# A diffusion-transformer trunk in float32: the last layer's second MLP product by Strassen's scheme of seven half products, with the residual transposed early and three of the products kept in PSUM

## The chip, the cores and the metric

The kernel runs on one core of a Trainium2 chip. A core has five engines with instruction streams of their own: PE (TensorE, the matrix unit), DVE (VectorE), ACT (ScalarE), POOL (GpSimd) and SP (SyncE, which here issues the DMAs). Tiles live in SBUF (128 partitions) and matmul results in PSUM. The metric is the device time of one execution in microseconds. The profile is that of one execution; its times are microseconds from its first instruction.

## The reference, cut to what matters

```python
def sqrelu_mlp(h, w1, w2):
    return jnp.square(jax.nn.relu(h @ w1)) @ w2
...
    for i in range(DEPTH):
        ...
        x = x + gx1 * y_x
        ...
        x = x + gx2 * sqrelu_mlp(modulate(rmsnorm(x, norm2_g[i]), sx2, ax2), w_mlp1[i], w_mlp2[i])
    return x
```

There are two layers, 512 latent tokens and a width of 1024; the MLP's hidden width is 4096. In the last layer only the latent tokens go through the MLP, and its result is the output (512 x 1024, token by row). The change lies in that last layer: in the product of the squared activations (512 x 4096) with `w_mlp2` (4096 x 1024), the gate `gx2` and the residual sum.

## The kernel before

Each product is taken in float32 accuracy from three matmuls. An operand is split into a high part, rounded to the matrix unit's format (`split`: ACT copies it, line 76), and a low part, the rest (DVE or POOL subtracts, line 77). Then high x high, high x low and low x high are added in PSUM (`mm3`, lines 109 to 111; `fm_block` runs it over the depth). A weight slab is a 1 MB DMA on SP into a raw tile (`r_w`, `load_slab`, line 90), then two ACT copies of 128x1024 into `h_w` and two subtractions of 128x1024 into `l_w`. The pool of these high and low parts has two buffers each.

The activations `X` are kept feature by partition, token by column. The last layer's MLP goes over the hidden width in four chunks of 1024. For each chunk:

- `hidden`, the first product (tiles `f`): four slabs of 256 hidden features, each two blocks of 24 matmuls with 512 tokens as columns. ACT takes relu (L1250), the square as high part `fh` (L1251) and the square (L1252), DVE the low part `fl` (L1253).
- `out_slabs`, the second product (tiles `r`): four slabs of 256 output features, each two blocks of 24 matmuls; the weights are the stationary operand. DVE adds gate x result to `X` (L1171).

So a chunk is 192 matmuls of `f` and 192 of `r`, and PE goes from one to the other without a pause. In the last layer the low parts of these weights are taken by DVE; POOL is not used in this MLP once the second norm is done. In the last chunk each `r` slab is followed by `after`: eight transposes to token by row (tiles `oT`, L1306), copies by DVE and ACT, and four DMAs to the output (L1313).

The first chunk begins while the second norm (`norm_mod`) is still at work on the second half of the tokens: ones-matmul `nc_n` (L331) sums the squares over partitions, DVE and POOL make the factor (`ms_n`, `dg_n`), the matmul `nb_n` (L320) spreads it, and from this DVE, ACT and POOL make the normed half (`nu_n`, `h2h`, `h2l`). Slabs 0 and 1 of the first chunk are therefore computed in halves of 256 tokens, the first halves of both slabs first:

```python
for s0 in ((0, 2), (2, 3), (3, 4)) if cch == 0 else ((n, n + 1) for n in range(4)):
    ...
    for g in halves if cch == 0 and s0[0] == 0 else groups:
```

The program is written as straight code; a scheduler places each instruction in its engine's stream, and an engine works its stream in order.

## Time and profile before

| | |
|---|---|
| three runs of the kernel before | 2336.35, 2337.66 and 2341.13 us, median 2337.66 |
| span of the profiled execution | 2337.3 us |
| granted clock of PE in it | 0.994 |
| last layer's MLP, first `f` matmul to the span's end | 1973.13 to 2337.3 us |
| last `r` phase, first matmul to the span's end | 2284.85 to 2337.3 us |

In a row of the timeline the columns are the start, the length, the engine, the line, the operation, and output <- inputs by the program's names; "xN" joins N like rows, whose length is then that from the first one's start to the last one's end. In brackets stands the time that the engine was idle before it, and what ended that. In a grouped row the columns behind the bar are busy us and mean ns of one, then the idle time ahead of the group. A matmul's length is that of its whole way through the array: the next one starts before it ends, so the distance from start to start is what one costs. In the table of windows each engine has its busy time with the number of its instructions in brackets, and behind them stand PE's granted clock, DMA's busy share and GB/s.

### The profile page before, as it was taken

The numbers are of one execution on the slowest core, as the hardware profiler recorded it, in microseconds if no ns is written. First come the engines' busy times: TensorE is split into PE (matmuls) and PEld (weight loads), VectorE is DVE, ScalarE is ACT, GpSimd is POOL, SyncE is SP. The second block draws the span as 40 slices with busy tenths as digits, with TensorE's granted clock in tenths as the row PEclk, the third lists the DMA queues.
The fourth block names the chain that finished last, engine by engine and source line by source line (L and its number), as shares of the span: only waits on it lengthen the run. The fifth ranks groups of instructions, "written<-read, shape, count | busy, mean of one in ns | idle before, by whom it ended". The sixth has DMA issues, their size and how long they took to land.

```text
span 2337.3 us, 36377 instructions
## 1 busy us (share of the span) xinstructions
PE 2272.6 (97%) x14626; PEld 2036.2 (87%) x14626; DVE 1488.6 (64%) x2586; ACT 996.0 (43%) x1967; POOL 681.8 (29%) x789
## 2 busy tenths in 40 slices
PE   8999999999999999999999999999999999999999
PEld 6999998888888998888888998999877779888887
DVE  6777776599657445555656567867759965433333
ACT  5555655522333362332415255655543334432432
POOL 1866764110000143232323266757510000000000
PEclk9999999999999999999999999999999999999999
DMA  9211111134544223333334311111114324223222
GB/s 305 61 36 45 46 46 45 46 129 142 175 139 165 65 82 120 124 109 126 122 113 128 108 46 57 44 44 44 62 41 160 115 88 127 90 91 106 92 91 72
DMA packets 222570, 224.76 MB, mean 96 GB/s; under 512 B 6256, under 2 KB 212544, under 8 KB 222272
## 3 DMA queue, kind: packets, MB, share of 16 engines
q1 hardware_dynamic: 222400, 222.43, 29.5%
q8 instruction: 115, 1.88, 0.3%
q14 instruction: 55, 0.45, 0.1%
HBM read 208.73 MB, written 13.67 MB: 95 GB/s over the span
## 4 chain that ended last, share of the span: by engine, by line
PE 78%; DVE 11%; POOL 4%; ACT 3%; DMA 2%; issue 2%; SPq 0%; POOLq 0%; DVEq 0%; ACTq 0%
PE r L109 6%; PE r L111 6%; PE r L110 6%; PE f L109 6%; PE f L110 6%; PE f L111 6%; DVE cacc L974 3%; PE qk L109 2%; PE qk L110 2%; PE qk L111 2%; PE gt L109 2%; PE gt L110 2%; PE gt L111 2%; PE o L109 2%; PE o L110 2%
## 5 line engine op out<-in xcount | busy, mean ns | idle before, releaser
L110 PE MATMUL f<-h2l,h_w 128*128 128x512 f32 (+1 forms) x832 | 282.7, 341 | 1.3 <-POOL h2l L77 1.3
L109 PE MATMUL f<-h2h,h_w 128*128 128x512 f32 (+1 forms) x832 | 281.7, 342 | 2.2 <-ACT h2h L76 1.7
L109 PE MATMUL r<-fh,h_w 128*128 128x512 f32 (+1 forms) x832 | 283.2, 341 | 0.1
L110 PE MATMUL r<-fl,h_w 128*128 128x512 f32 (+1 forms) x832 | 283.0, 340 | 0.0
L111 PE MATMUL r<-fh,l_w 128*128 128x512 f32 (+1 forms) x832 | 282.9, 340 | 0.0
L111 PE MATMUL f<-h2h,l_w 128*128 128x512 f32 (+1 forms) x832 | 281.3, 340 | 0.0
L77 POOL TENSOR_TENSOR l_w<-r_w,h_w 128x1024 fp32r<-128x1024 f32 x64 | 157.1, 2476 | 336.8 <-ACT h_w L76 336.8
L76 ACT ACTIVATE h_w<-r_w 128x1024 fp32r<-128x1024 f32 x128 | 128.6, 1052 | 225.4 <-PE r L110 117.2
L974 DVE SCALAR_TENSOR_TENSOR cacc<-z,cols,cacc 128x783 f32<-128x783 f32 (+1 forms) x240 | 207.8, 917 | 0.3
L1171 DVE SCALAR_TENSOR_TENSOR X<-r,ad,X 128x512 f32<-128x512 f32 (+1 forms) x104 | 65.1, 626 | 190.3 <-PE r L111 190.0
L109 PE MATMUL qk<-h_wqk,h1h 128*128 128x256 f32 x640 | 183.3, 289 | 2.1 <-ACT rw L566 1.3
L110 PE MATMUL qk<-l_wqk,h1h 128*128 128x256 f32 x640 | 180.7, 285 | 0.0
L111 PE MATMUL qk<-h_wqk,h1l 128*128 128x256 f32 x640 | 176.9, 285 | 0.3 <-POOL h1l L77 0.3
L1253 DVE TENSOR_TENSOR fl<-fr,fh 128x512 fp32r<-128x512 f32 (+1 forms) x104 | 77.3, 746 | 155.7 <-ACT fr L1252 155.5
L110 PEld LDWEIGHTS f<-h2l,h_w 128*128 128x128 f32 x832 | 157.5, 189 | 20.1 <-POOL h2l L77 2.4
L109 PEld LDWEIGHTS f<-h2h,h_w 128*128 128x128 f32 x832 | 156.6, 189 | 21.1 <-ACT h2h L76 2.3
L109 PEld LDWEIGHTS r<-fh,h_w 128*128 128x128 f32 x832 | 157.7, 190 | 17.7 <-DVE X L1171 0.3
L111 PEld LDWEIGHTS r<-fh,l_w 128*128 128x128 f32 x832 | 157.7, 190 | 17.7
L110 PEld LDWEIGHTS r<-fl,h_w 128*128 128x128 f32 x832 | 157.8, 190 | 17.4
L111 PEld LDWEIGHTS f<-h2h,l_w 128*128 128x128 f32 x832 | 157.2, 189 | 17.6
L738 DVE TENSOR_REDUCE st<-S 128x1 f32<-128x768 f32 (+1 forms) x160 | 134.4, 845 | 57.9 <-PE S L736 56.7
L279 DVE SCALAR_TENSOR_TENSOR adaac<-ar,cvec,adaac 128x256 f32<-128x256 f32 x336 | 156.5, 529 | 20.4 <-ACT adaac L276 15.5
(256 smaller groups left out, 6281.8 us busy)
## 6 DMA issues: line engine op xcount, KB each, us to landing
r_w<-in_w_mlp_dram SPq DMA_DIRECT2D x64, 1024.0 KB, 5.3
ada<-in_w_ada_dram SPq DMA_DIRECT2D x24, 1024.0 KB, 5.6
ar<-in_w_ada_dram SPq DMA_DIRECT2D x48, 512.0 KB, 3.6
r_wqk<-in_w_in_dram SPq DMA_DIRECT2D x32, 512.0 KB, 5.1
r_wg<-in_w_in_dram SPq DMA_DIRECT2D x16, 1024.0 KB, 5.4
r_wv<-in_w_in_dram SPq DMA_DIRECT2D x8, 1024.0 KB, 5.2
r_wao<-in_w_attn_out_dram SPq DMA_DIRECT2D x8, 1024.0 KB, 4.8
r_wo<-in_w_out_dram SPq DMA_DIRECT2D x8, 1024.0 KB, 8.8
```

The source lines that it names most:

```text
L76: nc.scalar.activation(out=hi, in_=src, func=AF.Copy)
L77: return (lo_eng or nc.vector).tensor_tensor(out=lo, in0=src, in1=f32(hi), op=ALU.subtract)
L109: nc.tensor.matmul(ps, sh, mh, start=first, stop=False)
L110: nc.tensor.matmul(ps, sh, ml, start=False, stop=False)
L111: nc.tensor.matmul(ps, sl, mh, start=False, stop=last)
L279: nc.vector.scalar_tensor_tensor(out=a[:, q], in0=r[:, j], scalar=cvec[:, k, q : q + 1], in1=a[:, q], op0=ALU.mult, op1=ALU.add)
L738: nc.vector.tensor_reduce(out=st[:, m : m + 1], in_=S[:, :nkey], axis=AX.X, op=ALU.max, negate=True)
L974: nc.vector.scalar_tensor_tensor(out=ca[cc][:, :CV], in0=zt[cc][:, t : t + CV], scalar=wcol, in1=ca[cc][:, :CV], op0=ALU.mult, op1=ALU.add)
L1171: state["done"] = nc.vector.scalar_tensor_tensor(out=X[:, mb, g], in0=ps[:, :W], scalar=gate[:, s, mb : mb + 1], in1=X[:, mb, g], op0=ALU. ...
L1253: state["done"] = nc.vector.tensor_tensor(out=fl[mb][:, g], in0=r[:, :W], in1=f32(fh[mb][:, g]), op=ALU.subtract).ins
```

## The change

For the last layer a new function `last_mixing` takes the place of the loop over chunks. A chunk's second product is A (512 tokens x 1024 hidden) times B (1024 hidden x 1024 outputs). Both are cut in two by two: A11, A12, A21, A22 are halves by tokens and by hidden features (each slab's first block of 128 goes to the first half, its second to the second), and B's quarters `b11`, `b12`, `b21`, `b22` are loaded by one 1 MB DMA each (rows of 512 columns, four raw buffers). Instead of eight half products there are seven, in the Winograd form: with S1 = A21 + A22, S2 = S1 - A11, S3 = A11 - A21, S4 = A12 - S2 and T1 = b12 - b11, T2 = b22 - T1, T3 = b22 - b12, T4 = b21 - T2 they are product 1 = A11 b11, 2 = A12 b21, 3 = S4 b22, 4 = A22 T4, 5 = S1 T1, 6 = S2 T2 and 7 = S3 T3. Their order is 1, 5, 6, 3, 7, 2, 4. Each is two blocks (128 tokens each) of 24 matmuls of 512 columns, so a chunk has 168 matmuls in place of 192. The activations are now the stationary operand, and the result comes out token by row.

- DVE makes the four sums of activations for each slab (`sm`, 128x256 each, L500 to L503) and the low parts of A11 (`aol`) and of the second block (in `h2hl`, unused columns of the old `h2l` tile); ACT copies the high parts, and POOL subtracts the low parts of the four sums (128x1024).
- DVE makes T1 (L559), T2 (L561), T3 (L562) and T4 (L564) in the raw tiles, 128x2048 each.
- `halves_of` splits each of the seven right operands: ACT copies two halves of 128x1024, DVE subtracts the first half and POOL the second.
- Products 1, 5, 6 and 7 are added over the chunks into quarters of `X` (L533, after the first chunk with one operand in PSUM); 3, 2 and 4 stay in PSUM over the four chunks.
- The residual `X` is transposed in the first chunk (`turn_x`, 32 transposes at L476, copies at L480 and L482, eight DMAs of 256 KB to `xt_d`) and read back at the end; the gate comes as a row for all partitions (`grow`) through DRAM.
- At the end DVE joins the products (L590 to L608), applies the gate (L586) and adds the residual (L587), POOL does the latter two for one quarter, and the last quarter is done in `u` tiles (L616, L617; three buffers) of 256 columns. The outputs go out by ten DMAs (L546, L618).
- In the first chunk only slab 0 is computed in halves of 256 tokens, and block by block instead of half by half.

What the function replaces in the chunk loop (`after` with its transposes and `out_slabs` for the last layer) is left out of the diff:

```diff
+    def last_mixing(fp, mi_, mc, X, h2, h2hl, L, w1):
...
+        def turn_x(n):
+            t, h = n // 2, n % 2
+            ps = mi_.tile([P, 512], F32, tag="mi", name=f"xT{n}")
+            for k in range(4):
+                nc.tensor.transpose(ps[:, k * P : k * P + P],
+                                    X[:, 4 * h + k, t * P : t * P + P], ident)
+            o = state["xp"].tile([P, 512], F32, tag="u", bufs=3, name=f"xt{n}")
...
+            nc.sync.dma_start(xt_d[t, h], o)
+
+        def hidden(c, s):
...
+            for m in range(2):
+                for g in (LAT,) if c or s else (slice(0, 256), slice(256, 512)):
...
+                    nc.scalar.activation(out=fr[:, m, g], in_=ps[:, :W], func=AF.Relu)
+                    nc.scalar.activation(out=fr[:, m, g], in_=fr[:, m, g], func=AF.Square)
+            sm = fp.tile([P, 4, HP], F32, tag="sm", name=f"sm{c}_{s}")
+            a11, a21, a12, a22 = fr[:, 0, :HP], fr[:, 0, HP:], fr[:, 1, :HP], fr[:, 1, HP:]
+            tt = nc.vector.tensor_tensor
+            split(AB[0][:, 0, s], AB[1][:, 0, s], a11)
+            tt(out=sm[:, 0], in0=a21, in1=a22, op=ALU.add)
+            tt(out=sm[:, 2], in0=a11, in1=a21, op=ALU.subtract)
+            tt(out=sm[:, 1], in0=sm[:, 0], in1=a11, op=ALU.subtract)
+            tt(out=sm[:, 3], in0=a12, in1=sm[:, 1], op=ALU.subtract)
+            split(AT[0][:, :, s], AT[1][:, :, s], fr[:, 1].rearrange("p (o n) -> p o n", o=2))
+            split(AB[0][:, 1:, s], AB[1][:, 1:, s], sm, nc.gpsimd)
+
+        def quarter(c, kh, nh):
+            r = fp.tile([P, HK, HN], F32, tag="raw", bufs=4, name=f"r_w2_{c}_{kh}{nh}")
...
+        def halves_of(r, name):
+            hi = wpool.tile([P, HK, HN], F32R, tag="whi", name=f"h_{name}")
+            lo = wpool.tile([P, HK, HN], F32R, tag="wlo", name=f"l_{name}")
+            for k, eng in ((slice(0, 2), nc.vector), (slice(2, 4), nc.gpsimd)):
+                split(hi[:, k], lo[:, k], r[:, k], eng)
+            return hi, lo
+
...
+        tt = nc.vector.tensor_tensor
+        kept = {}
+
+        def summed(n, c, a, w):
+            for t in range(2):
+                ps = mm_tile(f"r{c}_{n}_{t}")
+                product(ps, a, w, t, True, True)
+                if c:
+                    tt(out=M[n][:, t], in0=M[n][:, t], in1=ps, op=ALU.add)
+                else:
+                    nc.vector.tensor_copy(M[n][:, t], ps)
+
+        def held(n, c, a, w, t):
+            if c == 0:
+                pool, tg = (mc, "mc") if n == 2 else (mi_, "mi")
+                kept[n, t] = pool.tile([P, 512], F32, tag=tg, name=f"r_{n}_{t}")
+            product(kept[n, t], a, w, t, c == 0, c == 3)
+            return kept[n, t]
+
...
+        quarters = Y.rearrange("p t (h n) -> p h t n", h=2)
+        M = {n: quarters[:, q // 2, 2 * (q % 2) : 2 * (q % 2) + 2]
+             for q, n in enumerate((1, 5, 6, 7))}
+        for c in range(4):
+            for s in range(4):
+                hidden(c, s)
+                if c == 0:
+                    turn_x(2 * s)
+                    turn_x(2 * s + 1)
+            b22, b12, b21, b11 = (quarter(c, *q) for q in ((1, 1), (0, 1), (1, 0), (0, 0)))
+            summed(1, c, A11, halves_of(b11, f"b11_{c}"))
+            tt(out=b11, in0=b12, in1=b11, op=ALU.subtract)
+            summed(5, c, S1, halves_of(b11, f"t1_{c}"))
+            tt(out=b11, in0=b22, in1=b11, op=ALU.subtract)
+            tt(out=b12, in0=b22, in1=b12, op=ALU.subtract)
+            summed(6, c, S2, halves_of(b11, f"t2_{c}"))
+            tt(out=b11, in0=b21, in1=b11, op=ALU.subtract)
+            w22 = halves_of(b22, f"b22_{c}")
+            if c < 3:
+                for t in range(2):
+                    held(3, c, S4, w22, t)
+                summed(7, c, S3, halves_of(b12, f"t3_{c}"))
+                w21 = halves_of(b21, f"b21_{c}")
+                for t in range(2):
+                    held(2, c, A12, w21, t)
+                wt4 = halves_of(b11, f"t4_{c}")
+                for t in range(2):
+                    held(4, c, A22, wt4, t)
+                continue
+
+            gn = [grow[:, :HN], grow[:, HN:]]
+            xt = []
+            for q in range(2):
+                r = fp.tile([P, 2, 2, 512], F32, tag="raw", bufs=4, name=f"xr{q}")
+                nc.sync.dma_start(r, xt_d[2 * q : 2 * q + 2].rearrange("t h p n -> p t h n"))
+                xt.append(r)
+
+            def gated(tq, nq, t, v, eng=nc.vector):
+                eng.tensor_tensor(out=v, in0=v, in1=gn[nq], op=ALU.mult)
+                eng.tensor_tensor(out=v, in0=v, in1=xt[tq][:, t, nq], op=ALU.add)
+
+            for t in range(2):
+                tt(out=M[6][:, t], in0=M[1][:, t], in1=M[6][:, t], op=ALU.add)
+            for t in range(2):
+                ps = held(3, c, S4, w22, t)
+                v = state["xp"].tile([P, 512], F32, tag="u", bufs=3, name=f"c12_{t}")
+                tt(out=v, in0=M[5][:, t], in1=ps, op=ALU.add)
+                tt(out=v, in0=M[6][:, t], in1=v, op=ALU.add)
+                gated(0, 1, t, v)
+                put(0, 1, t, v)
+            summed(7, c, S3, halves_of(b12, f"t3_{c}"))
+            for t in range(2):
+                tt(out=M[7][:, t], in0=M[6][:, t], in1=M[7][:, t], op=ALU.add)
+                tt(out=M[5][:, t], in0=M[7][:, t], in1=M[5][:, t], op=ALU.add)
+                gated(1, 1, t, M[5][:, t], nc.gpsimd)
+                put(1, 1, t, M[5][:, t])
+                gated(1, 0, t, M[7][:, t])
+            w21 = halves_of(b21, f"b21_{c}")
+            for t in range(2):
+                ps = held(2, c, A12, w21, t)
+                tt(out=M[1][:, t], in0=M[1][:, t], in1=ps, op=ALU.add)
+                gated(0, 0, t, M[1][:, t])
+                put(0, 0, t, M[1][:, t])
+            wt4 = halves_of(b11, f"t4_{c}")
+            for t in range(2):
+                ps = held(4, c, A22, wt4, t)
+                for j, o in enumerate((slice(0, 256), slice(256, 512))):
+                    u = state["xp"].tile([P, 512], F32, tag="u", bufs=3, name=f"u{t}_{j}")[:, :256]
+                    tt(out=u, in0=ps[:, o], in1=gn[0][:, o], op=ALU.mult)
+                    tt(out=u, in0=u, in1=M[7][:, t, o], op=ALU.add)
+                    nc.sync.dma_start(out[0, (2 + t) * P : (3 + t) * P, o], u)
...
```

Where the change moves instructions, three places show it. First, the product phase of the second chunk. On DVE, before, in the phase of the third chunk (names: `l_w2` low parts of the weights, `fl` low parts of the activations, `r` the second product's blocks):

```order
L77 TENSOR_TENSOR l_w2_1_2_0_22193<-r_w2_1_2_0_22190,h_w2_1_2_0_22192 128x1024 x2
L1253 TENSOR_TENSOR fl1_2_5_21913<-fr1_2_5_0_22117,fh1_2_5_21912 128x512
L1253 TENSOR_TENSOR fl1_2_6_21915<-fr1_2_6_0_22155,fh1_2_6_21914 128x512
L77 TENSOR_TENSOR l_w2_1_2_1_22253<-r_w2_1_2_1_22250,h_w2_1_2_1_22252 128x1024 x2
L1253 TENSOR_TENSOR fl1_2_7_21917<-fr1_2_7_0_22185,fh1_2_7_21916 128x512
L1171 SCALAR_TENSOR_TENSOR X2_20128<-r1_2_0_0_22198,ad1_9372,X2_20128 128x512
L1171 SCALAR_TENSOR_TENSOR X2_20128<-r1_2_1_0_22224,ad1_9372,X2_20128 128x512
L77 TENSOR_TENSOR l_w2_1_2_2_22313<-r_w2_1_2_2_22310,h_w2_1_2_2_22312 128x1024 x2
L1171 SCALAR_TENSOR_TENSOR X2_20128<-r1_2_2_0_22258,ad1_9372,X2_20128 128x512
```

and after, in the phase of the second chunk (`r_w2_1_00`, `01`, `10`, `11` are the raw quarters b11, b12, b21, b22, overwritten by T1, T2, T4 in the first and T3 in the second; `fr1_3` are slab 3's activations, `r1_n_t` a block of product n):

```order
L503 TENSOR_TENSOR sm1_2_21606<-fr1_2_21551,sm1_2_21606 128x256
L559 TENSOR_TENSOR r_w2_1_00_21697<-r_w2_1_01_21693,r_w2_1_00_21697 128x2048
L562 TENSOR_TENSOR r_w2_1_01_21693<-r_w2_1_11_21691,r_w2_1_01_21693 128x2048
L77 TENSOR_TENSOR aol_20749<-fr1_3_21625,aoh_20748 128x256
L501 TENSOR_TENSOR sm1_3_21680<-fr1_3_21625 128x256
L77 TENSOR_TENSOR l_t1_1_21735<-r_w2_1_00_21697,h_t1_1_21734 128x1024
L533 TENSOR_TENSOR X2_20130<-X2_20130,r1_1_0_21705 128x512
L500 TENSOR_TENSOR sm1_3_21680<-fr1_3_21625 128x256
L502 TENSOR_TENSOR sm1_3_21680<-sm1_3_21680,fr1_3_21625 128x256
L77 TENSOR_TENSOR h2hl1_20141<-fr1_3_21625,h2hh1_20140 128x2x256
L503 TENSOR_TENSOR sm1_3_21680<-fr1_3_21625,sm1_3_21680 128x256
L561 TENSOR_TENSOR r_w2_1_00_21697<-r_w2_1_11_21691,r_w2_1_00_21697 128x2048
```

Where DVE had one subtraction of the weights and one gated sum per block, it now has sums of 128x2048, and T3 (the row of L562) stands ahead of slab 3's low part `aol` and its sums. On POOL, whose last row before was a low part of the second norm, ahead of this MLP's chunks, there are now eleven subtractions of 128x1024 a chunk, here those of the second chunk from b11 on:

```order
L77 TENSOR_TENSOR l_b11_1_21700<-r_w2_1_00_21697,h_b11_1_21699 128x1024
L77 TENSOR_TENSOR aol_20749<-sm1_2_21606,aoh_20748 128x4x256
L77 TENSOR_TENSOR l_t1_1_21735<-r_w2_1_00_21697,h_t1_1_21734 128x1024
L77 TENSOR_TENSOR aol_20749<-sm1_3_21680,aoh_20748 128x4x256
L77 TENSOR_TENSOR l_t2_1_21771<-r_w2_1_00_21697,h_t2_1_21770 128x1024
L77 TENSOR_TENSOR l_b22_1_21806<-r_w2_1_11_21691,h_b22_1_21805 128x1024
L77 TENSOR_TENSOR l_t3_1_21836<-r_w2_1_01_21693,h_t3_1_21835 128x1024
L77 TENSOR_TENSOR l_b21_1_21870<-r_w2_1_10_21695,h_b21_1_21869 128x1024
L77 TENSOR_TENSOR l_t4_1_21900<-r_w2_1_00_21697,h_t4_1_21899 128x1024
```

The low parts of the activation sums (`sm1_2`, `sm1_3`, of slabs 2 and 3) stand between those of b11, t1 and t2.

Second, the start of the MLP on PE (`f1_0_b` is block b of the first chunk, its first half of the tokens). Before, the matmul `nc_n` came behind the two blocks of slab 0, and `nb_n` 35 matmuls later, in the last of slab 1's two:

```order
L110 MATMUL f1_0_1_0_20788<-h2l1_20139,h_w1_1_0_0_20623 128x256
L111 MATMUL f1_0_1_0_20788<-h2h1_20138,l_w1_1_0_0_20624 128x256
L331 MATMUL nc_n2_1_256_20695<-cst_75,acc1_2_20129 128x1 x2
L109 MATMUL f1_0_2_0_20818<-h2h1_20138,h_w1_1_0_1_20689 128x256
L110 MATMUL f1_0_2_0_20818<-h2l1_20139,h_w1_1_0_1_20689 128x256
```

After, both come behind one block, with no work between them, and twelve of the early transposes `xT` follow:

```order
L110 MATMUL f1_0_0_0_0_20754<-h2hl1_20141,h_w1_1_0_0_20625 128x256
L111 MATMUL f1_0_0_0_0_20754<-h2hh1_20140,l_w1_1_0_0_20626 128x256
L334 MATMUL nc_n2_1_256_20697<-cst_75,acc1_2_20131 128x1 x2
L323 MATMUL nb_n2_1_256_20706<-dg_n2_1_256_20703,cst_75 128x256
L476 MATMUL xT0_20873<-cst_75,X2_20130 128x128 x4
L476 MATMUL xT1_20881<-cst_75,X2_20130 128x128 x4
L476 MATMUL xT2_20955<-cst_75,X2_20130 128x128 x4
L109 MATMUL f1_0_0_0_256_20781<-h2hh1_20140,h_w1_1_0_0_20625 128x256
L109 MATMUL f1_0_0_1_0_20808<-h2hh1_20140,h_w1_1_0_0_20625 128x256
L110 MATMUL f1_0_0_1_0_20808<-h2hl1_20141,h_w1_1_0_0_20625 128x256
```

The blocks `f1_0_0_0_256` (first block, second half) and `f1_0_0_1_0` (second block, first half) are then mixed.

Third, the end on DVE. Before, the last rows were the gated sum of the last two blocks and two copies of transposed ones:

```order
L1312 COPY ot2_0_22949<-oT2_0_22946 128x256
L1312 COPY ot2_2_22961<-oT2_2_22958 128x256
L1171 SCALAR_TENSOR_TENSOR X2_20128<-r1_3_6_0_22978,ad1_9372,X2_20128 128x512
L1171 SCALAR_TENSOR_TENSOR X2_20128<-r1_3_7_0_23004,ad1_9372,X2_20128 128x512
L1312 COPY ot3_0_23033<-oT3_0_23030 128x256
L1312 COPY ot3_2_23045<-oT3_2_23042 128x256
```

After (`r_4_t` is product 4's block in PSUM, `X2` holds the joined products), these stand behind 28 operations of 512 columns from product 6 on:

```order
L587 TENSOR_TENSOR X2_20130<-X2_20130,xr1_22881 128x512
L586 TENSOR_TENSOR X2_20130<-X2_20130,grow_20750 128x512
L587 TENSOR_TENSOR X2_20130<-X2_20130,xr0_22879 128x512 x2
L616 TENSOR_TENSOR u0_0_23025<-r_4_0_21369,grow_20750 128x256
L616 TENSOR_TENSOR u0_1_23029<-r_4_0_21369,grow_20750 128x256
L616 TENSOR_TENSOR u1_0_23045<-r_4_1_21382,grow_20750 128x256
L617 TENSOR_TENSOR u0_0_23025<-u0_0_23025,X2_20130 128x256
L617 TENSOR_TENSOR u0_1_23029<-u0_1_23029,X2_20130 128x256
L617 TENSOR_TENSOR u1_0_23045<-u1_0_23045,X2_20130 128x256
L616 TENSOR_TENSOR u1_1_23049<-r_4_1_21382,grow_20750 128x256
L617 TENSOR_TENSOR u1_1_23049<-u1_1_23049,X2_20130 128x256
```

The fourth `u1_1` takes the buffer of `u0_0`, the first of three.

More of the change, by code (lines that the diff above doesn't have):

```diff
@@ L1161, in trunk_kernel @@
         xp = xpool.__enter__()
[L1162 to L1163 removed]
+        X = xp.tile([P, KT, nv], F32, tag="X", name=f"X{i + 1}")
+        acc = xp.tile([P, nv], F32, tag="acc", name=f"acc{i}_2")
         state["xp"] = xp
@@ L1208, in out_slabs @@
                     after(3)
-        h2h = hpool.tile([P, KT, NT], F32R, tag="hh", name=f"h2h{i}")
-        h2l = hpool.tile([P, KT, NT], F32R, tag="hl", name=f"h2l{i}")
+        h2 = [hpool.tile([P, KT * NT], F32R, tag=tg, name=f"h2{tg}{i}") for tg in ("hh", "hl")]
+        h2h, h2l = (t[:, : KT * nv].rearrange("p (k n) -> p k n", k=KT) for t in h2)
         def norm2(g):
@@ L1237, in ada_step @@
         def ada_step():
-            if not last:
-                with tc.issue_after(state["done"]):
-                    next(ada_todo, None)
-        for cch in range(4):
+            with tc.issue_after(state["done"]):
+                next(ada_todo, None)
+        if last:
+            gpool.__exit__(None, None, None)
+            gpool = tc.tile_pool(name="fpool", bufs=1, reuse_waits="tile")
+            gp = gpool.__enter__()
+            last_mixing(gp, mi_, mc, X, h2, (h2h, h2l), L, w1)
+        for cch in () if last else range(4):
             fh, fl = [None] * KT, [None] * KT
@@ L1270, in trunk_kernel @@
             fin = cch == 3
-            if fin and not last:
+            if fin:
                 drain(ada_todo)
@@ L1298, in after @@
             def after(s):
-                if fin and not last:
+                if fin:
                     nc.sync.dma_start(xs_d[i + 1][:, 2 * s : 2 * s + 2, :],
                                       X[:, 2 * s : 2 * s + 2, :])
-                if fin and last:
-                    for t in range(4):
-                        ps = state["mi"](f"oT{s}_{t}")
-                        for m in range(2):
-                            nc.tensor.transpose(ps[:, m * P : m * P + P],
-                                                X[:, 2 * s + m, t * P : t * P + P], ident)
-                        ot = gp.tile([P, 512], F32, tag="t2k", bufs=4, name=f"ot{s}_{t}")
-                        if t % 2:
-                            nc.scalar.activation(out=ot[:, :256], in_=ps[:, :256], func=AF.Copy)
-                        else:
-                            nc.vector.tensor_copy(ot[:, :256], ps[:, :256])
-                        nc.sync.dma_start(out[0, t * P : t * P + P, 256 * s : 256 * s + 256],
-                                          ot[:, :256])
             out_slabs(
@@ L1318, in trunk_kernel @@
                     w_mlp2[i][1024 * cch : 1024 * cch + 1024, 256 * s : 256 * s + 256]
-                    .rearrange("(k p) n -> p k n", p=P), f"w2_{i}_{cch}_{s}", lo_eng=None if last else nc.gpsimd),
+                    .rearrange("(k p) n -> p k n", p=P), f"w2_{i}_{cch}_{s}", lo_eng=nc.gpsimd),
                 lambda k: (fh[k], fl[k]), gate2, f"r{i}_{cch}",
-                norm1 if fin and not last else None, after, tick=ada_step, ahead=
+                norm1 if fin else None, after, tick=ada_step, ahead=
                 (lambda: first.update(w=qk_slab(i + 1, 0, nc.gpsimd)),
-                 v_first) if fin and not last else ())
+                 v_first) if fin else ())
         if not last:
```

36 lines of the change are left out of this document (34 added, 2 removed).

## The prediction, made before the changed kernel was run

> **What bounds the kernel now.** I read the page's first part, then the stage table of the last layer's MLP, then its grouped lines, then the rows at each stage's edges.
>
> ```profile
> PE 2272.6 (97%) x14626; PEld 2036.2 (87%) x14626; DVE 1488.6 (64%) x2586; ACT 996.0 (43%) x1967; POOL 681.8 (29%) x789
> ```
> ```profile
> core 0: us, PE busy (x) PEld busy (x) DVE busy (x) ACT busy (x) POOL busy (x), PEclk, DMA share, GB/s
> 1973.00:2023.70 50.70, 48.09 (x297) 42.49 (x296) 26.57 (x47) 31.13 (x66) 7.20 (x9) 1.00 0.30 99
> 2023.70:2067.30 43.60, 43.60 (x194) 36.08 (x193) 15.39 (x16) 9.87 (x12) 0.00 (x0) 1.00 0.30 97
> 2285.00:2337.30 52.30, 47.43 (x225) 38.97 (x223) 16.90 (x23) 10.24 (x17) 0.00 (x0) 0.98 0.18 61
> ```
>
> The columns after the stage's length are the busy time of PE, its weight loads, DVE, ACT and POOL. The row from 2023.70 is one chunk's second product (`r`): PE is busy for all of it at a granted clock of 1.00, DVE for a third, POOL for none. PE sets the pace there, so each matmul taken out is worth its pitch, as long as DVE and POOL can feed it. The pitch is in the rows at the edges:
>
> ```profile
> 2023.73 0.39 PE L109 MATMUL r<-fh,h_w 128*128 128x512 f32 x1
> ...
> 2067.26 0.39 PE L109 MATMUL f<-h2h,h_w 128*128 128x512 f32 x1
> ...
> 2284.85 0.39 PE L109 MATMUL r<-fh,h_w 128*128 128x512 f32 x1
> ...
> 2330.95 0.39 PE L111 MATMUL r<-fh,l_w 128*128 128x512 f32 x1
> ```
>
> 192 matmuls take 2067.26 - 2023.73 = 43.53 us, 0.2268 us each (0.39 is one's modelled length in the pipeline). The last `r` phase starts at 2284.85, and the span ends 52.45 us later.
>
> **The change part by part.** It removes 24 of 192 matmuls in each of four chunks: 96 x 0.2268 = 21.8 us of PE. A chunk's product phase then holds 168 x 0.2268 = 38.1 us. The order on PE holds these 168, so the removal is real. What is added is on DVE and POOL; the prices:
>
> ```profile
> L77 DVE TENSOR_TENSOR l_w<-r_w,h_w 128x1024 fp32r<-128x1024 f32 x62 | 73.2, 1221 | 58.4 <-ACT h_w L76 56.8
> L76 ACT ACTIVATE h_w<-r_w 128x1024 fp32r<-128x1024 f32 x62 | 62.3, 1052 | 161.4 <-PE r L110 113.5 <-PE f L110 47.9
> L1253 DVE TENSOR_TENSOR fl<-fr,fh 128x512 fp32r<-128x512 f32 x28 | 19.4, 693 | 52.2 <-ACT fr L1252 52.2
> L1253 DVE TENSOR_TENSOR fl<-fr,fh 128x256 fp32r<-128x256 f32 x8 | 3.3, 421 | 3.4 <-ACT fr L1252 3.4
> L640 POOL TENSOR_TENSOR dupc<-rwc,gr 128x512 f32<-128x512 f32 x8 | 10.3, 1294 | 5.6 <-DVE rwc L637 5.6
> ```
>
> Behind each bar stand busy time and mean ns of one. From 421 to 1221 ns over 768 elements an element costs 1.04 ns on DVE; back to back, some 0.08 us of each is overlapped. So I price DVE at 0.35 us (256 elements), 0.62 (512), 1.14 (1024), and the new sums of 128x2048 at 2.25 (between 2.2 and twice 1.22; the trace has none). ACT's 1024 elements cost 1.05, POOL's 512 cost 1.25. Each chunk adds four 2048-long sums of weight quarters, four sums of activations per slab, and on POOL seven 128x1024 low parts and four of the activation sums. By busy time alone DVE would have room: in a product phase POOL has some 19 us of work and DVE some 24, of 38. What decides is whether they can work at once. These rows show it:
>
> ```profile
> 1474.26 3.26 DVE L77 TENSOR_TENSOR l_wqk<-r_wqk,h_wqk 128x1024 fp32r<-128x1024 f32 x1
> ```
> ```profile
> 1474.04 2.39 POOL L77 TENSOR_TENSOR l_wqk<-r_wqk,h_wqk 128x1024 fp32r<-128x1024 f32 x1 [0.87 <-ACT h_wqk L76]
> ```
> ```profile
> 816.40 1.48 DVE L358 TENSOR_TENSOR acc<-acc,nsq_so 128x256 f32<-128x256 f32 x1 [1.41 <-ACT nsq_so L357]
> 817.80 0.47 DVE L1171 SCALAR_TENSOR_TENSOR X<-o,ad,X 128x256 f32<-128x256 f32 x1
> ```
> ```profile
> 815.19 4.94 POOL L77 TENSOR_TENSOR l_w<-r_w,h_w 128x1024 fp32r<-128x1024 f32 x2 [1.05 <-ACT h_w L76]
> ```
>
> The first DVE row does what the 1.22 us group does, but takes 3.26 us: it starts 0.22 us behind a POOL subtraction of 2.39 us and ends 1477.52, 1.09 us after POOL's end at 1476.43. So it stood still until POOL was done. At 816.40 a sum that costs 0.42 takes 1.48 beside two POOL subtractions: it ends at 817.88, about 0.2 us after the middle of their 4.94 us, so it got in between the two. The next row reads one operand from PSUM, lies inside POOL's second subtraction, and is not slowed (0.47). I read: **POOL's two-operand work on SBUF and DVE's two-operand work on SBUF exclude each other whole, and take turns**; POOL's 1024 elements cost 2.36.
>
> The Trainium skill, "SBUF — State Buffer", section "Who interferes with whom", says the same: a DVE instruction with two SBUF inputs contends with a GpSimd instruction that reads SBUF, and the later one blocks fully. The trace agrees (3.26 us). The Trainium skill, "Advanced Engine Details and Errata", section "VectorE Performance Modes", speaks otherwise: it ties the blocking to DVE's two-port modes, and the first page says in the same section that an operation on two tensors has none. By the first page the sum is as below; by the second's sentence alone the engines would run side by side, which is rival A. The 3.26 us row speaks against that.
>
> **A product phase** (0 = end of the last hidden slab on PE). The high parts have two buffers, so ACT copies b11's when slab 2 (10.9 us before the end) has done with one: from -10.9, two copies of 1.05, done at -8.7. From there this must go one after another, as DVE's and POOL's orders above show, until product 3 (b22) can begin its second matmul: on POOL the low halves of b11, t1, t2, b22 and the activation sums of slabs 2 and 3, 6 x 2.36 = 14.2; on DVE T1, T3, T2, T4, 4 x 2.25 = 9.0, three low halves, 3 x 1.14 = 3.4, eight small sums and lows of 256, 8 x 0.35 = 2.8, two lows of 512, 1.2, and one evacuation from PSUM between them, 0.6. Sum 31.2, so it ends at 22.5, with hand-offs 22.9. PE alone would be there after 73 matmuls, at 16.6. **PE therefore waits 6.3 us a chunk**, some at product 1 for slab 3's low part (queued on DVE behind T3 and POOL's low part of t1), some at product 5 for the low parts of the sums, the rest at product 3. After that each further pair of halves (3.5 us) fits within a product (5.4 us). The phase takes 38.1 + 6.3 = 44.4 against 43.53: +0.9 a chunk, +2.7 over three. The hidden slabs have room: 10.9 us each on PE, against one POOL item of 2.36 and some 4.5 us of DVE.
>
> **The start.** Before, four first-half blocks of slabs 0 and 1 covered the norm of the second half; now one does, of slab 0 alone.
>
> ```profile
> 1975.47 0.28 PE L111 MATMUL f<-h2h,l_w 128*128 128x256 f32 x1
> ...
> 1981.90 0.61 PE L331 MATMUL nc_n<-cst,acc 128*128 128x1 f32 x4
> ...
> 1986.64 0.59 PE L320 MATMUL nb_n<-dg_n,cst 128*128 128x256 f32 x2
> ```
> ```profile
> 1983.57 0.48 DVE L316 TENSOR_SCALAR dg_n<-cst,ms_n 128x128 f32<-128x128 f32 x2
> ...
> 1987.27 1.26 DVE L338 SCALAR_TENSOR_TENSOR nu_n<-X,A,nb_n 128x256 f32<-128x256 f32 x3
> ```
> ```profile
> 1994.32 0.74 POOL L77 TENSOR_TENSOR h2l<-nu_n,h2h 128x256 fp32r<-128x256 f32 x1 [1.02 <-ACT h2h L76]
> ```
>
> `nc_n` waits for the sums of squares, which the change leaves as they are, so it stays at 1981.9, and PE, with one block instead of two before it and none behind it, idles. `nb_n` follows when `dg_n` is done, at 1984.1 instead of 1986.64. In the old trace the second half's last low part ended 8.4 us after `nb_n` began (1995.06): now about 1992.5. From 1984.1 PE has 72 matmuls of 256 columns (0.12 each, the step from row to row, 8.6) and 28 early transposes:
>
> ```profile
> 2331.18 0.60 PE L1306 MATMUL oT<-cst,X 128*128 128x128 f32 x4
> ```
>
> Four transposes end 0.60 after the first begins, 0.27 of it one's own: 0.11 each, 3.1 in all. Without a wait slab 0 ends at 1995.8; with a whole block and the tail of another behind 1992.5, up to 1999.5. I take 1997.5. Then 4 transposes and 144 x 0.2268 = 32.7 bring the first product at 2030.6 instead of 2023.73: **+6.9** (5.2 to 8.9). The transposes are in this number; the 24 that ran within the old last phase are in its 52.45. ACT and DVE copy them in slab 0, eight DMAs take them away, none waited for before the end.
>
> **The end.** In the last chunk DVE also does, from product 6 on, 28 operations of 512 columns (17.4 us) and three low halves (3.4): from 22.9 to 43.7 if nothing holds it. But three low halves and four gated operations on POOL (7.1 + 5.0) exclude most of them, and the residual rows read back land late; some 10.5 us are exposed, so DVE comes to the six first `u` operations at 54.2, while PE's last matmul is at about 48. The fourth `u` needs the first one's buffer of three, free once its DMA has landed:
>
> ```profile
> out_dram<-ot SPq DMA_DIRECT2D x16, 128.0 KB, 1.8
> ```
> ```profile
> 2333.00 1.81 SPq L1313 DMA_DIRECT2D out_dram<-ot  x4
> ```
>
> With a quarter of 1.81 for the issue, 2.3: DVE ends at 58.8, the last output lands at 61.1. Against 52.45: **+8.7**.
>
> Sum: 6.9 + 2.7 + 8.7 = +18.3 on the profiled span of 2337.3, so 2355.6. The median before lies 0.4 above that span: **2356**. The terms' bounds (start 2, sums and hand-offs 1 a phase, end 4) give its own range, 2347 to 2366. Quarter loads are in there too:
>
> ```profile
> DMA to landing us min/median/max: 4.7/5.3/6.9
> ```
>
> By the order on SP and of the buffers, b11's load can be issued some 7.5 us before ACT needs it; at 6.9 it is in time.
>
> **The rivals.** *A, faster: DVE and POOL run side by side.* Place: every product phase; it decides if a 128x1024 subtraction on DVE beside one on POOL stays near 1.2 us. For it speaks only POOL's and DVE's low busy share, against it 3.26 and 1.48 us. Then the only wait left is one for a PSUM buffer at product 5 (0.8): 38.9 a phase, -4.6 x 3 = -13.9; the last phase needs 38.9 + 6.3 for evacuation, `u` and DMA = 45.2, -7.2; with +6.9: -14.2, **2323**.
> *B: the exclusion lasts only while POOL reads, half of its time.* Then half of the waits remain: a phase of 41.6, -5.8 over three, the end (61.1 + 45.2) / 2 = 53.1, +0.7, start +6.9: +1.8, **2340**. Against it: the DVE operation at 1474.26 ended a full 1.09 after POOL's end.
> *C, slower: loads late.* A 1 MB load can take longer:
>
> ```profile
> r_wo<-in_w_out_dram SPq DMA_DIRECT2D x8, 1024.0 KB, 8.8
> ```
>
> At 8.8 b11 is 1.3 late four times, and the residual rows as much: +6.5, **2362**, inside the range.
>
> **How the numbers follow.** Forecast 0.68, A 0.12, B 0.14, C 0.06. A measurement of this kernel can tell some 0.2% from no change (4.7 us, 2333 to 2342). The forecast and C are slower, 0.74; B is the same, 0.14; A faster, 0.12. The range takes in the forecast's own and B's, and leaves A out: 2335 to 2366.
>
> **What would show it.** Right: DVE's weight subtractions and 2048-long sums beside a POOL subtraction take 3 to 5 us instead of 1.2 and 2.25; PE waits 5 to 7 us in each of the first three product phases, all before product 7, on low parts; the phases take 44 to 45 us; the first product begins near 2030; DVE is the last engine to compute, some 10 us behind PE's last matmul. Wrong: phases near 39 (A), or near 41.5 (B); waits on DMA (C); a first product before 2028.

## The result, and the profile after

The changed kernel took 2354.97 us (median of five runs, 2351.78 to 2356.54), the kernel before 2340.03 in the five runs taken so far (2336.35 to 2341.13): 1.0062 times as long, 95% interval 1.0050 to 1.0074. The forecast was 2356, slower. The profiled execution has a span of 2353.2 us at a mean clock of 0.988. First its line of engines, then the table of windows over the stages of this MLP: first `f` matmul to first product, the first and the second product phase, and the last one to the span's end.

```profile
PE 2258.8 (96%) x14482; PEld 2016.3 (86%) x14482; DVE 1582.8 (67%) x2686; ACT 1032.2 (44%) x1995; POOL 814.9 (35%) x837
```
```profile
core 0: us, PE busy (x) PEld busy (x) DVE busy (x) ACT busy (x) POOL busy (x), PEclk, DMA share, GB/s
1974.30:2033.80 59.50, 54.78 (x280) 47.37 (x279) 37.65 (x59) 34.97 (x65) 18.12 (x13) 0.89 0.44 149
2033.80:2077.10 43.30, 39.63 (x170) 31.15 (x170) 28.70 (x25) 16.88 (x18) 20.85 (x7) 1.00 0.33 99
2120.60:2163.80 43.20, 39.54 (x169) 31.13 (x168) 28.65 (x25) 16.86 (x18) 20.87 (x7) 1.00 0.32 101
2294.10:2353.20 59.10, 40.60 (x169) 30.71 (x167) 53.49 (x55) 14.85 (x16) 27.63 (x11) 0.91 0.21 71
```

PE issues 24 matmuls fewer in a product phase, and the phase is as long as before (43.2 against 43.5): what was taken out came back as waiting. DVE and POOL are busy 28.7 and 20.9 us there, where they were 15.4 and 0. From the starts of matmuls, stage by stage:

| stage | before, us | after, us | change | forecast of the change |
|---|---|---|---|---|
| span's start to the first `f` of this MLP | 1973.13 | 1974.34 | +1.2 | 0 |
| first `f` to first product | 50.6 | 59.5 | +8.9 | +6.9 |
| three product phases | 3 x 43.52 | 3 x 43.24 | -0.8 | +2.7 |
| three hidden phases | 3 x 43.52 | 3 x 43.52 | 0 | 0 |
| last product phase to the span's end | 52.4 | 59.1 | +6.7 | +8.7 |

The sum, +15.9, is the difference of the two spans (2353.2 - 2337.3). The first row lies outside the change: that point came at 1968.6 to 1977.4 in the profiles below, whatever was edited. Without it the stages add up to +14.8. The kernel before took 2335.0 to 2351.6 us over all its runs in these experiments, so the whole of one run says little within some 15 us; a stage that an edit leaves alone repeats within 0.3 us, so comparisons go by the lengths of stages.

Where PE waits in the second product phase of the changed kernel (rows of its timeline with an idle time ahead):

```profile
2127.23 0.50 PE L109 MATMUL r<-h_t,aoh 128*128 128x512 f32 x1 [0.98 <-DVE X L533]
2130.05 0.50 PE L109 MATMUL r<-h_t,aoh 128*128 128x512 f32 x1 [0.49 <-ACT aoh L76]
2131.76 0.50 PE L109 MATMUL r<-h_t,aoh 128*128 128x512 f32 x1 [0.97 <-DVE X L533]
2135.65 0.47 PE L109 MATMUL r<-h_t,aoh 128*128 128x512 f32 x1 [0.65 <-DVE X L533]
2142.40 0.50 PE L110 MATMUL r<-l_b,aoh 128*128 128x512 f32 x1 [0.57 <-DVE l_b L77]
```

Five waits; an idle time counts from a matmul's modelled end, so from start to start each costs more, and in all they make 5.1 us over the even pitch (6.3 forecast). A product is 24 matmuls, two blocks of 12 (not of 24 each, as the section on the change has it), so the first three waits lie in product 5, the fourth at the start of product 6 and the last in product 3. None comes after product 3, as forecast; none comes in product 1 either, where one was forecast. And three of the five end with DVE's L533, which empties the PSUM buffer of a finished block: PE waits there for a place to write to, not for an operand. A fourth is for a high part, which ACT copies late because DVE's sums come late. Only the last, at product 3, is for a low part. DVE is late with these because of what stands ahead of them. Some of its rows, and POOL's, from just before that phase:

```profile
2118.19 4.37 DVE L562 TENSOR_TENSOR r_w<-r_w,r_w 128x2048 f32<-128x2048 f32 x1
2122.48 0.41 DVE L77 TENSOR_TENSOR aol<-fr,aoh 128x256 fp32r<-128x256 f32 x1
2122.82 2.62 DVE L501 TENSOR_TENSOR sm<-fr 128x256 f32<-128x256 f32 x1
...
2126.50 0.68 DVE L533 TENSOR_TENSOR X<-X,r 128x512 f32<-128x512 f32 x1
...
2128.82 2.29 DVE L561 TENSOR_TENSOR r_w<-r_w,r_w 128x2048 f32<-128x2048 f32 x1
2131.03 0.68 DVE L533 TENSOR_TENSOR X<-X,r 128x512 f32<-128x512 f32 x1
```
```profile
2117.13 3.28 POOL L77 TENSOR_TENSOR aol<-sm,aoh 128x1024 fp32r<-128x1024 f32 x1 [2.86 <-ACT aoh L76]
2122.67 2.48 POOL L77 TENSOR_TENSOR l_t<-r_w,h_t 128x1024 fp32r<-128x1024 f32 x1 [2.26 <-ACT h_t L76]
2130.08 3.28 POOL L77 TENSOR_TENSOR aol<-sm,aoh 128x1024 fp32r<-128x1024 f32 x1 [4.92 <-ACT aoh L76]
```

T3 (L562) takes 4.37 us where T2 (L561) takes 2.29: it stands still until POOL's subtraction ends at 2120.41. A sum of 256 columns (0.41 alone) takes 2.62 and ends 0.3 behind POOL's next one. POOL's subtractions from 2117.13 and 2130.08 (2.4 alone) in turn waited for the ends of T1 and T2. What counts is where the operands lie, as predicted: L533, with one operand in PSUM, takes 0.68 at 2126.50, when POOL rests, and the same 0.68 at 2131.03, when T2 has ended and POOL is at work.

### The profile page after: what moved, and what is told of

It reads as the page before. It is cut to its first block, busy times and chain, and to the rows that moved or that the text cites. A ratio compares the mean times of both kernels' runs of the same rounds, so it can differ in the third digit from the quotient of the medians.

```text
span 2353.2 us, 36323 instructions
## 1 busy us (share of the span) xinstructions
PE 2258.8 (96%) x14482; PEld 2016.3 (86%) x14482; DVE 1582.8 (67%) x2686; ACT 1032.2 (44%) x1995; POOL 814.9 (35%) x837
## 4 chain that ended last, share of the span: by engine, by line
PE 72%; DVE 15%; POOL 5%; ACT 3%; DMA 3%; issue 2%; SPq 0%; POOLq 0%; DVEq 0%; ACTq 0%
PE f L110 6%; PE f L109 6%; PE f L111 6%; PE r L110 5%; PE r L111 5%; PE r L109 5%; DVE cacc L1140 3%; PE qk L109 2%; PE qk L110 2%; PE qk L111 2%; PE gt L109 2%; PE gt L110 2%; PE gt L111 2%; PE o L109 2%; PE o L110 2%
## 5 line engine op out<-in xcount | busy, mean ns | idle before, releaser
L109 PE MATMUL f<-h2hh,h_w 128*128 128x512 f32 (+1 forms) x816 | 281.6, 347 | 2.3 <-ACT h2hh L76 2.1
L110 PE MATMUL f<-h2hl,h_w 128*128 128x512 f32 (+1 forms) x816 | 281.0, 346 | 1.4 <-POOL h2hl L77 1.4
L111 PE MATMUL f<-h2hh,l_w 128*128 128x512 f32 (+1 forms) x816 | 279.3, 344 | 0.0
L109 PE MATMUL r<-fh,h_w 128*128 128x256 f32 (+1 forms) x576 | 183.7, 319 | 0.0
L110 PE MATMUL r<-fl,h_w 128*128 128x256 f32 (+1 forms) x576 | 183.4, 319 | 0.0
L111 PE MATMUL r<-fh,l_w 128*128 128x256 f32 (+1 forms) x576 | 183.3, 319 | 0.0
L109 PEld LDWEIGHTS f<-h2hh,h_w 128*128 128x128 f32 x816 | 155.1, 191 | 21.5 <-ACT h2hh L76 2.5
L110 PEld LDWEIGHTS f<-h2hl,h_w 128*128 128x128 f32 x816 | 155.2, 191 | 20.6 <-POOL h2hl L77 2.4
L111 PEld LDWEIGHTS f<-h2hh,l_w 128*128 128x128 f32 x816 | 155.2, 191 | 18.1
L109 PE MATMUL gt<-h1h,h_wg 128*128 128x512 f32 (+1 forms) x384 | 138.2, 360 | 0.0
```

Of the source, the lines that this page charges most:

```text
L109: nc.tensor.matmul(ps, sh, mh, start=first, stop=False)
L110: nc.tensor.matmul(ps, sh, ml, start=False, stop=False)
L111: nc.tensor.matmul(ps, sl, mh, start=False, stop=last)
```

## The experiments

In all of them the hidden phases stay at 43.52. "Phase" below is one of the first three product phases, "end" the last one to the span's end, "start" the stretch from first `f` to first product. Those told without a ratio to the kernel before are one execution each; their wholes, where not given below, are 2349.69 us (2), 2344.35 (5), 2358.78 (7) and 2356.07 (8).

**1. The cost by itself: the kernel before, with POOL given work.**

```diff
+        if name.startswith("w2_1"):
+            for k in (slice(0, half), slice(half, shape[0])):
+                x = state["tp"].tile([P, half, 256], F32R, tag="extra", name=f"x_{name}", bufs=1)
+                nc.gpsimd.tensor_tensor(out=x, in0=r[:, k], in1=f32(hi[:, k]), op=ALU.subtract)
```

> The kernel before, with two subtractions of 128x1024 on POOL added beside each slab's two on DVE in the last layer's second product (their result is not used). Theory (exclusion): DVE's low parts of the second product's weights, 1.22 us before, take 2 to 3.5 us each, while the gated sums (one operand from PSUM) stay at 0.75; DVE is busy a third of that stage, so PE waits for nothing and the phases stay at 43.5. Rival (no exclusion): DVE's low parts stay at 1.2 to 1.3.

The groups of its first `r` phase by line and shape (busy us and mean ns behind the bar):

```profile
L105 POOL TENSOR_TENSOR x_w<-r_w,h_w 128x1024 fp32r<-128x1024 f32 x6 | 19.9, 3322 | 12.7 <-issue 12.5
L77 DVE TENSOR_TENSOR l_w<-r_w,h_w 128x1024 fp32r<-128x1024 f32 x8 | 16.0, 2048 | 3.4 <-ACT h_w L76 3.4
L1175 DVE SCALAR_TENSOR_TENSOR X<-r,ad,X 128x512 f32<-128x512 f32 x7 | 5.3, 751 | 13.4 <-PE r L115 13.4
```

DVE's subtractions go from 1222 to 2048 ns on average. Three of the four pairs stand beside POOL's work and take 1.23 us (the one that starts first) and 3.41 to 3.43; the fourth, with POOL idle, takes 1.23 and 1.22. The gated sum with one operand in PSUM keeps its 751 ns to the nanosecond. The phase stays at 43.52 and the whole at 2336.11: the exclusion is there, and costs nothing where DVE has slack. So the theory holds with nothing else changed.

**2. POOL writes, but reads nothing.** The subtraction in the second half of each right operand becomes two memsets, 1.96 us together.

```diff
-            for k, eng in ((slice(0, 2), nc.vector), (slice(2, 4), nc.gpsimd)):
-                split(hi[:, k], lo[:, k], r[:, k], eng)
+            split(hi[:, :2], lo[:, :2], r[:, :2], nc.vector)
+            nc.scalar.activation(out=hi[:, 2:], in_=r[:, 2:], func=AF.Copy)
+            for _ in range(2):
+                nc.gpsimd.memset(f32(lo[:, 2:]), 0.0)
```

> The changed kernel, with POOL's subtraction of 128x1024 in each right operand replaced by two memsets of the same tile, which read nothing; the second half of each right operand's low part is then zero, so that much of the computation is left out, though every matmul is still there. Theory (exclusion by what is read from SBUF): DVE's sums and subtractions beside a memset keep their own 1.2 and 2.3 us, four POOL items leave the chain, and the first three phases take 38.5 to 40 us instead of 43.2. Rival (POOL at work is what slows DVE, or any shared write does): DVE's operations beside the memsets are still stretched to 2.5 to 4 us, and the phases stay above 42.

Operations were as the theory says: beside the memsets DVE's low halves take 1.23 us and T2, which overlaps one for 0.6 us, 2.28. The phases were not: 43.8, 43.4 and 43.8, the rival's number, though not for the rival's reason. Two rows of PE and POOL in the second phase show the first part of why:

```profile
2132.67 1.09 PE L111 MATMUL r<-h_t,aol 128*128 128x512 f32 x2 [2.06 <-POOL aol L77]
```
```profile
2129.45 3.17 POOL L77 TENSOR_TENSOR aol<-sm,aoh 128x1024 fp32r<-128x1024 f32 x1 [2.96 <-ACT aoh L76]
```

The scheduler had set another order: the last sum of slab 3's activations stands behind T2 on DVE, so POOL's low part of these sums began late, waited for T4 and ended 13.5 us into the phase (12.8 in the changed kernel), and product 5 waited for it. Some waits went and another took their place. The second part is the clock: behind this wait some matmuls come every 0.43 us instead of 0.23, and the granted clock is 0.96 in all three phases, where the changed kernel has 1.00. That makes some 1.6 us a phase; without it the phases would be at about 42.2, an estimate, and so 1 us shorter, not the 3 to 5 expected. The end fell from 59.1 to 54.5.

**3. All low halves of the right operands on DVE.**

```diff
-            for k, eng in ((slice(0, 2), nc.vector), (slice(2, 4), nc.gpsimd)):
+            for k, eng in ((slice(0, 2), nc.vector), (slice(2, 4), nc.vector)):
```

> The changed kernel, with the second half of each right operand's low part subtracted by DVE instead of POOL: seven operations of 128x1024 a chunk go from the engine with little to do to the busier one. Theory (POOL's and DVE's two-operand work exclude each other): each costs the shared chain 1.14 us instead of 2.36, so of the 5.1 us that PE waits in a product phase 1 to 2.5 are left; the first three phases take 39.2 to 41 us instead of 43.2, the last phase to the span's end 51 to 55 instead of 59.1, the whole 2337 to 2345. Rival (DVE's sheer load or POOL's slowness, side by side): POOL's half was hidden beside DVE's, 8 us more for DVE a phase make the phases 45 us or longer, and the whole 2362 or more.

2364.26 us (1.0098 of the kernel before, 1.0068 to 1.0128), phases of 47.2, 46.0 and 47.3: the rival's numbers again. The rows of PE with a wait, and some of those behind them:

```profile
2130.41 0.50 PE L109 MATMUL r<-h_t,aoh 128*128 128x512 f32 x1 [1.74 <-DVE X L533]
2135.23 0.73 PE L111 MATMUL r<-h_t,aol 128*128 128x512 f32 x2 [1.55 <-POOL aol L77]
2137.98 0.73 PE L109 MATMUL r<-h_t,aoh 128*128 128x512 f32 x1 [2.02 <-DVE X L533]
2139.36 0.63 PE L109 MATMUL r<-h_t,aoh 128*128 128x512 f32 x1
2139.79 0.63 PE L110 MATMUL r<-l_t,aoh 128*128 128x512 f32 x1
```

The same displaced sum: POOL's low part for product 5 ends at 2135.2, 14.2 us into the phase. And behind three waits in ten us the matmuls come every 0.43 us instead of 0.23, for about 3 us: the clock in this phase is 0.96 (0.93 in the other two). So neither theory as stated: DVE was busy 31 us of 46, no bound by load. The displaced sum points to the order on DVE ahead of what PE needs next; the next two experiments set that order.

**4. One operation moved: T3 behind b22's low half.**

```diff
-            tt(out=b12, in0=b22, in1=b12, op=ALU.subtract)
...
             w22 = halves_of(b22, f"b22_{c}")
+            with tc.issue_after(state["half"]):
+                tt(out=b12, in0=b22, in1=b12, op=ALU.subtract)
```

> The changed kernel, with the sum T3 = b22 - b12 issued on DVE behind the low half of b22 instead of right behind T1. Theory (one exclusive chain of DVE and POOL sets the wait before product 3): 2.3 us leave the chain ahead of product 3, the first three phases take 40.5 to 41.8 us instead of 43.2, and most of the wait for slab 3's low part in product 1 goes. Rival (the waits are set by ACT's copies or by PSUM buffers): the phases stay within 0.5 us of 43.2.

Phases of 41.2 three times, as the theory has it: the length of one 128x2048 sum (2.3 us) moved off the way to product 3 brings 2.0 us. The first two waits in product 5 went; the three others stayed. The end fell by 1.1; the whole was 2342.09.

**5. The third experiment in order**: T3 later, all low halves on DVE, and T2 held behind slab 3's last sum.

```diff
-            tt(out=sm[:, 3], in0=a12, in1=sm[:, 1], op=ALU.subtract)
+            state["sums"] = tt(out=sm[:, 3], in0=a12, in1=sm[:, 1], op=ALU.subtract).ins
...
-            tt(out=b11, in0=b22, in1=b11, op=ALU.subtract)
+            with tc.issue_after(state["sums"]):
+                tt(out=b11, in0=b22, in1=b11, op=ALU.subtract)
```

> The kernel with T3 later, and with the second half of each right operand's low part subtracted by DVE instead of POOL, as in the first experiment, but with T2 held behind the last sum of slab 3's activations, so that DVE's order stays that of the changed kernel. Theory (one exclusive chain, where POOL's half costs 2.36 us and DVE's 1.14; the first experiment was spoilt by the sums that moved behind T2): the first three phases take 39 to 40.2 us, against 41.2 with T3 later alone, though DVE does 8 us more in each. Rival (POOL's half was hidden, and DVE's load counts): 42 us or more.

Neither range was met in full: 40.3 us in the first phase, 41.9 in the other two. The waits are the same in all three (for the last low part of product 5, and for the PSUM buffer of product 6); in the second and third phases seven matmuls behind them come at 0.43 us, at a granted clock of 0.96 where the first phase has 1.00. Against 41.2 with POOL's half, the first phase gains 0.9 us although DVE has seven more subtractions to do (some 8 us), so POOL's half had not been hidden. In the other two the clock took back more than that.

**6. The start as before.** Slabs 0 and 1 of the first chunk again in halves, the first halves of both ahead; the transposes stay.

```diff
-                for g in (LAT,) if c or s else (slice(0, 256), slice(256, 512)):
...
+            early = {} if c else squares(c, (0, 1), (slice(0, 256), slice(256, 512)))
             for s in range(4):
-                hidden(c, s)
+                hidden(c, s, early.get(s))
```

> The changed kernel, with slabs 0 and 1 of the first chunk again in halves of 256 tokens, the first halves of both first, as before; the 32 early transposes stay. Theory (too little work for PE ahead of the second half's norm; the wait also takes the clock down, which was 0.50 from 1978 to 1990 in the changed kernel): the stretch from the first f matmul to the first product takes 53.5 to 55 us instead of 59.5 (50.6 before and 3.5 for transposes), the clock in it stays at 1.00, the other stages stay. Rival (the transposes, their copies and their DMAs hold the start up): it stays above 57.

```profile
1972.90:2025.20 52.30, 50.48 (x329) 45.64 (x328) 37.43 (x59) 34.36 (x70) 17.65 (x13) 1.00 0.49 170
```

52.3 us instead of 59.5, at a clock of 1.00, with all 32 transposes (3.5 us of PE) in it: they cost 1.7 net against the kernel before (50.6). So of the +8.9 at the start 7.2 are the missing cover and 1.7 the transposes. The whole was 2346.38, all other stages as in the changed kernel.

**7. PE kept busy at the start**: in the changed kernel, 80 transposes of a constant in the gaps.

```diff
+                            for d in range(8 if k < KT - 1 else 24):
+                                nc.tensor.transpose(keep[:, 128 * (d % 4) : 128 * (d % 4) + 128],
+                                                    ident, ident)
```

> The changed kernel with 80 transposes of a constant on PE in the gaps of the first block of slab 0 and before the second half's norm (their result is not used). Theory (PE's waits there take its clock to one half, and that costs some 3 us of the start): the clock stays at 1.00 from 1975 to 2030 though PE does 9 us more, and the stretch from the first f matmul to the first product takes 55.5 to 57.5 us instead of 59.5. Rival (only the missing cover counts, the clock falls for another reason): 59.5 or more, or a clock that still falls.

```profile
1977.30:2037.60 60.30, 58.67 (x360) 51.81 (x360) 38.13 (x59) 34.85 (x67) 17.85 (x13) 1.00 0.43 148
```

The clock stayed at 1.00, so it had fallen because PE waited; but the stretch did not get shorter (60.3), and the theory's price falls. The extra work put `nc_n` off by 1.9 us. Behind it the full clock gives back 1.1: from `nc_n` to `nb_n` it is 2.2 us here and 3.0 with the half clock, from `nb_n` to the first product 47.5 and 47.8. So the half clock cost about 1.1 us of the start, not 3; what the start lacks above all is cover.

**8. The gated operations of quarter (1,1) on DVE.**

```diff
-                gated(1, 1, t, M[5][:, t], nc.gpsimd)
+                gated(1, 1, t, M[5][:, t])
```

> The changed kernel, with the four gated operations of the output quarter (1,1) on DVE instead of POOL. Theory (exclusion: they cost DVE's backlog 1.25 us each on POOL and 0.62 on DVE): the last phase to the span's end takes 56 to 57.5 us instead of 59.1, all else as in the changed kernel. Rival (POOL did them beside DVE): 61 us or more.

The end took 56.9 us instead of 59.1: four operations fewer on POOL, and DVE, which does them now, is done earlier.

**9. These together**, and slab 3's low parts of the sums on DVE as well.

```diff
-            split(AB[0][:, 1:, s], AB[1][:, 1:, s], sm, nc.gpsimd)
+            state["sums"] = split(AB[0][:, 1:, s], AB[1][:, 1:, s], sm,
+                                  nc.gpsimd if s < 3 else nc.vector).ins
```

> The changed kernel with the old start, T3 later, every low part of a right operand and slab 3's low parts of the activation sums on DVE, T2 held behind those, and the gated operations on DVE: POOL works only in the hidden slabs. Theory (exclusive chain and clock): first f matmul to first product 52.3 us, the first three phases 38.9 to 40 us with the clock at 1.00 in them, the last phase to the end 50 to 53, so 2326 to 2331 where the kernel before takes 2337 to 2340. Rival (DVE, which now has some 34 of 38 us to do in a phase, is the new bound): phases of 42 us or more and an end of 57 or more, 2340 or slower.

2336.62 us, 0.9976 of the kernel before (0.9962 to 0.9990); 2326 to 2331 was expected. The start met its number (52.3); the phases (40.6, 42.2, 42.2) and the end (54.2) did not. DVE is busy 31.3 us in a phase, so its load is no bound, against the rival. Holding T2 behind slab 3's low parts had made T2 itself late, and behind it the emptying of product 5's buffers (L542) and the low half that product 6 needs:

```profile
2123.67 0.74 PE L109 MATMUL r<-h_t,aoh 128*128 128x512 f32 x2 [1.38 <-DVE X L542]
2124.93 0.51 PE L110 MATMUL r<-l_t,aoh 128*128 128x512 f32 x1 [0.52 <-DVE l_t L77]
```

Two waits within 1.3 us, and again seven matmuls at 0.43 us behind them in the second phase and the third.

**10. Product 2 in second place.** It needs no sum, so the sums get the time of one product. Its `held` further down goes, and the `u` operations are held behind the last gated ones.

```diff
             summed(1, c, A11, halves_of(b11, f"b11_{c}"))
+            w21 = halves_of(b21, f"b21_{c}")
+            two = [held(2, c, A12, w21, t) for t in range(2)]
```

> The kernel with all of the former edits together, and product 2, which needs no sum, moved from the sixth place to the second (its result waits in PSUM as before), so that the sums have 5.4 us more before PE needs them; the u operations of the end stand behind the last gated ones. Theory (what stands on DVE ahead of the low parts that PE needs next sets the waits, and two waits close together take the clock down): the 1.5 and 0.7 us waits at product 6 go, the clock stays at 1.00, the first three phases take 38.2 to 39.5 us instead of 40.6 to 42.2, the last phase to the end 48 to 52, and the whole 2321 to 2328. Rival (DVE's load, some 35 of 38 us a phase, is the bound): phases of 40.5 us or more, 2333 or slower.

```profile
2027.30:2066.30 39.00, 38.45 (x169) 31.44 (x169) 31.45 (x31) 16.79 (x18) 0.00 (x0) 1.00 0.35 109
2109.80:2148.80 39.00, 38.46 (x170) 31.44 (x170) 31.44 (x31) 16.77 (x18) 0.04 (x1) 1.00 0.35 109
2274.80:2330.80 56.00, 38.54 (x169) 31.22 (x167) 48.50 (x65) 14.72 (x16) 0.00 (x0) 0.87 0.21 75
```

The phases take 38.95 us, 0.85 over their 168 matmuls, at a clock of 1.00; one wait is left, for T2's low half at product 6. DVE at 31.4 us of 39 is no bound. The whole is 2331.16 us, **0.9945 of the kernel before** (0.9927 to 0.9963), the fastest here, but not the 2321 to 2328 expected. Its end missed the expectation (56.0, not 48 to 52): PE issues its last matmul 38.7 us into the last phase, and the span ends 17.3 us later, behind DVE's joins, gates and residual (48.5 us of DVE in that phase). Whether that end can be made shorter was not tried further.

## Why the prediction was right, point by point

- **Slower: right**, by 14.8 us in the stages that the change touches, where 18.3 was forecast, and for the reasons given. The largest part, +8.9, is the start: its lost cover, and 1.7 of early transposes. In the phases and at the end it is that POOL's and DVE's work with two operands in SBUF exclude each other; experiment 1 shows this alone, and in the changed kernel the phases lost in waits nearly all that the matmuls had saved. That 2356 lies within 1 us of the measured median is partly luck: the stages were off by +2.0, -3.5 and -2.0, and the stretch ahead of them took 1.2 longer in the profile.
- **The product phase: mechanism right, size off.** 5.1 us of waits against 6.3, a phase of 43.2 against 44.4, so -0.8 in place of +2.7. The term that was too large is the chain of 31.2 us: b22's low half ended 21.7 us into the phase, not 22.9. Where the waits fall was mostly wrong: the prediction has them all on low parts, beginning in product 1; one of five is on a low part, one on a high part, three on PSUM buffers that DVE empties late, and none is in product 1. The total could come out all the same, because the last wait, at product 3, ends when the chain does.
- **The reasoning about that chain was too simple.** It counts durations up to product 3, as if any of them taken out came off the phase. Experiments 2 and 3 took POOL's half out and gained nothing, since the scheduler then set another order, another product waited, and the clock fell behind that wait. Where the order was set by hand the phases got shorter: T3 moved alone brought 2.0 us of the 5.1 (4), POOL's half on DVE 0.9 more at full clock (5), and product 2 moved took 1.6 off experiment 9's first phase (10). That the order counts as much was not in the prediction. No run takes the exclusion away with both the order and the clock held, so its own share of the 5.1 us stays open.
- **The start: mechanism right, 2.0 us short** (8.9 against 6.9). The measured value lies at the upper bound that was given (8.9). The missing cover is shown by experiment 6. The step that was too small is the one from `nc_n` to the end of slab 0: `nb_n` came 3.0 us behind `nc_n`, not 2.2, and slab 0 ended 14.6 behind `nb_n`, not 13.4. A granted clock of 0.50 through most of 1978 to 1990 was not foreseen; in experiment 7, where it stays at 1.00, 1.1 of the 2.0 are gone, among them the 0.8 between `nc_n` and `nb_n`.
- **The end: mechanism right, 2.0 us too long** (59.1 against 61.1). DVE is the last to compute, 11 us behind PE's last matmul. The first `u` begins 52.4 us into the phase, not 54.2; 1.1 of that is b22's low half again (21.8 against 22.9), the rest the estimate of 10.5 us exposed. Residual rows that land late were part of that estimate, and no row of DVE waits for them. The fourth `u` waits 1.17 us for a DMA, as foreseen:

```profile
2349.74 0.42 DVE L616 TENSOR_TENSOR u<-r,grow 128x256 f32<-128x256 f32 x1 [1.17 <-DMA out_dram<-u]
```

- **Rival A** (2323) did not occur: the two engines do not run side by side here. That its phase of 38.9 is what experiment 10 measured is luck: A's 0.8 us is a wait for a PSUM buffer at product 5, and what is left in experiment 10 is a wait for an operand at product 6. Rivals B and C did not occur either: DVE's stretched operations end behind POOL's, and no wait of PE in the phases ends with a load.

## What to carry to other kernels

Work on GpSimd beside VectorE ran in parallel here only where VectorE read one operand from PSUM (0.68 and 0.75 us unchanged) or GpSimd read nothing (a memset); GpSimd reading one operand was not tried. Price two-operand work otherwise as if both were one engine, at GpSimd's slower rate (2.4 us for 128x1024 against 1.2). Before trusting a chain of durations, ask what the next late item is: on an in-order engine it is the order ahead of the next operand, or of the next PSUM evacuation, that sets the wait, and a scheduler may change it with every edit. A product that needs nothing new is cover for operands that are still being made: moving one took the phases from 40.6 and 42.2 us to 39.0.
